# S5 input side by pairs of f tiles, a three-step scan, the skip term on GpSimd, and weight buffers that join the end of the rotation

## The chip, the cores and the metric

One core of a Trainium2 chip runs the whole program in one launch. The metric is device time in microseconds (us); smaller is better. The engines are named as in the profile: PE is TensorE (PEld its weight load), DVE is VectorE, ACT is ScalarE, POOL is GpSimd, and SP issues most DMAs.

## What is computed

Two layers, a gated linear attention (GLA) layer and an S5 layer, on 256 tokens of width 2048, all in float32. The change lies mainly in the S5 layer, whose mixer is, cut to what matters:

```python
proj = u_in @ w_in                      # (256, 2048) @ (2048, 8192)
u, z = jnp.split(proj, 2, axis=-1)      # 256 groups of 16 channels each
# per group g, with 64 complex states and step dt:
lb = exp(a * dt)                        # diagonal transition
bb = (lb - 1) / a * b                   # 64 x 16 input matrix
x[l] = lb * x[l-1] + bb @ u[l]          # complex recurrence along the tokens
y[l] = real(c @ x[l])
y = y + d_skip * u
y = gelu(y)
y = y * sigmoid(y @ w_glu + b_glu)      # (256, 4096) @ (4096, 4096)
out = (y * silu(z)) @ w_out             # (256, 4096) @ (4096, 2048)
```

Around it stand the shift, scale and gate made from the vector c, and a LayerNorm of `ALPHA * x + gate * mixer` after each layer.

## The kernel before, in words

**Dense products.** Each weight comes in blocks of 256 x 512 (`wload`, 512 KB, issued on SP). `split` makes a high part on ACT (`hi`, a rounded copy) and a low part on DVE (`lo = w - hi`), and three fp32r matmuls (hi x hi, hi x lo, lo x hi) stand for one float32 product. The stages of the dense work, by the names of their PSUM tiles, are in this order: v and q (to 377 us of the span), z (377 to 591), op of layer 0 (591 to 771), su (the first half of the S5 `w_in`, 777 to 1052), sz (its second half, 1052 to 1322), gl (`w_glu`, 1325 to 1686), op of layer 1. A group g of su or sz is 512 output columns: four PSUM banks, 8 weight blocks (kp), 192 matmuls of 256 columns.

**Weight buffers.** `ring` is a list of buffer makers. `wload` takes the first and puts it at the end. Four belong to the pool `w`; a phase adds buffers of its own from its temporary pool `tp` (`ring_tmp`), at the front of the list. A pool that is opened where another was closed uses the same memory, so its first tiles wait for the last readers of the closed one's. hi and lo parts have three buffers each.

**The S5 side work** runs between the matmuls of su and sz. An f tile is 8 groups of 16 channels, and there are 32. The recurrence is cut in blocks of 8 tokens:
- `b_pow(f)`: DVE makes the powers of lb times bb (three operations of 128 x 896), from `rb[f // 2]`, which one load brings for two f.
- `b_tr(f)`: eight transposes on PE, copied by ACT to `wbt`.
- `s_in(f)`: a DVE transpose of the su bank, two PE transposes (`psu`), an ACT copy to `U`.
- `s_mm(f)`: eight small float32 matmuls U x wbt (L1014, 32 output partitions each), a DVE transpose of their result into the state array `sx`, then eight more small matmuls c x powers (L1024) into the other half of the same bank, copied by ACT to `kT`.
- `k_out(f)`: two PE transposes (`psk`), an ACT copy to `ks`, on DVE the diagonal skip term `dm` and its sum into `ks`, and a write to the DRAM table `dk` from POOL.
- `scan(c, h)`: one step of the recurrence from block to block, for one half h of the f tiles: four DVE operations of 128 x 128, 30 steps for each half.
- In sz: `cunit(f)` makes two factors wc0 and wc1 (for f % 8 >= 5 DVE adds them to one, L1109), `xstage(f)` transposes the state, and `ystage(f)` sums on PE: eight matmuls with `mt` from `dk`, and eight with each factor of wc.

PSUM has a pool `mm` of five banks for the dense products and `ax` of three for all the rest. `bstep` and `pump` bring in the side work at rates per weight block, and a scheduler then sets the order of the instructions on each engine when the program is built. Each engine and each DMA queue runs its list in that order.

Of the kernel before, what the change touches and what calls it, by code (L numbers as in the profile page):

```python
# [15 lines left out]
P = 128  # L16
# [17 lines left out]
def trunk(ctx, tc, x, c, ln_g, ln_b, ada_w, ada_b, gla_w_in, gla_gate_w2, gla_gate_b, gla_norm_g,  # L34
# [33 lines left out]
    rp.open("rows0")  # L68
    tp = Phase()
# [13 lines left out]
    ones = cp.tile([P, P], F32, name="ones")  # L83
    V.memset(ones, 1.0)
# [18 lines left out]

    last_lo = [None]

    def split(w, name):
        hi = hp.tile([P, 1024], F32R, tag="hi", name="hi" + name)
        lo = lp.tile([P, 1024], F32R, tag="lo", name="lo" + name)
# [10 lines left out]
    def ring_tmp(n):  # L119
        bufs = [lambda name: tp.tile([P, 1024], F32, tag="wx", name=name, bufs=n)] * n  # L120
        ring_add(bufs)
        return bufs[0]

    def ring_drop(buf):
        ring[:] = [b for b in ring if b is not buf]

    def wload(src, k0, c0, name, last=False):
        if last:
            w = wp.tile([P, 1024], F32, tag="w", name="w" + name)
        else:  # L130
            ring.append(ring.pop(0))
            w = ring[-1]("w" + name)
        dma(w.rearrange("p (k c) -> p k c", k=2),
            src[k0 * P:(k0 + 2) * P, c0:c0 + 512].rearrange("(k p) c -> p k c", p=P))
        return w

    def split_last(w, name, i):


        hi = (hp.tile([P, 1024], F32R, tag="hi", name="hi" + name) if i % 2 else lp.tile([P, 1024], F32R, tag="lo", name="hi" + name))  # L140
# [256 lines left out]
    early = ring_tmp(2)  # L397
# [9 lines left out]
    l8r = cp.tile([P, 128], F32, name="l8r")  # L407
    l8i = cp.tile([P, 2, 128], F32, name="l8i")
# [32 lines left out]
    def prep_lambda():  # L441
# [186 lines left out]
    SPLIT = 5  # L628
# [114 lines left out]
    ring_drop(early)  # L743
    tp.close()
    tp.open("tmp0b")
    mid = ring_tmp(4)
# [154 lines left out]
    ring_add(spare)  # L901
# [71 lines left out]
    wu, kts = {}, {}  # L973

    def b_pow(f):
        if f % 2 == 0:
            bload(f // 2)
        a = rb[f // 2][:, f % 2]

        w = tp.tile([P, 8, 16, 8], F32, tag="wu", name=f"wb{f}", bufs=2)  # L980
# [8 lines left out]
        wu[f] = w  # L989

    def b_tr(f):
        wt = tp.tile([P, 8, 128], F32, tag="wbt", name=f"wbt{f}", bufs=2)
        for h in range(2):
            ps = psx(f"pswb{f}{h}")
            for g in range(4):
                PE.transpose(ps[:, g * P:(g + 1) * P], wu[f][:, 4 * h + g].rearrange("p i s -> p (i s)"), ident)
            S.copy(wt[:, 4 * h:4 * h + 4, :], ps.rearrange("p (g r) -> p g r", g=4))
        wb[f] = wt

    def s_in(f, ps):  # L1000
# [8 lines left out]
    def s_mm(f):
        U = Ut[f // 8][:, f % 8]  # L1010
        pss = psx(f"pss{f}")
        for b in range(2):
            for q in range(4):
                PE.matmul(pss[32 * q:32 * q + 32, b * P:(b + 1) * P], lhsT=U[:, b, 32 * q:32 * q + 32],  # L1014
                          rhs=wb[f][:, 2 * q + b, :], start=True, stop=True)
        n = 2 * (f % 16)
        V.transpose(sx[:, f // 16, 1:33, :, n:n + 2].rearrange("p c r b -> p b r c"),
                    pss[:, :T].rearrange("p (b r l) -> p b r l", b=2, r=4))

        cc = rb[f // 2][:, f % 2]  # L1020
        for b in range(2):
            for q in range(4):
                g = 2 * q + b
                PE.matmul(pss[32 * q:32 * q + 32, T + b * P:T + (b + 1) * P], lhsT=cc[:, g * 16:g * 16 + 32],  # L1024
                          rhs=wu[f][:, g].rearrange("p i n -> p (i n)"), start=True, stop=True)
        kt_ = tp.tile([P, 2, P], F32, tag="kt", name=f"kT{f}", bufs=2)
        S.copy(kt_.rearrange("p b (n i) -> p b n i", n=8), pss[:, T:].rearrange("p (b i n) -> p b n i", b=2, i=16))
        kts[f] = kt_

    def k_out(f):  # L1030
        kt_ = kts[f]
        pk_ = psx(f"psk{f}")
        for b in range(2):
            PE.transpose(pk_[:, b * P:(b + 1) * P], kt_[:, b], ident)
        pk = pk_[:, :T].rearrange("p (b q i) -> p q b i", b=2, q=4)[:, :, :, :16]
        ks = tp.tile([P, P], F32, tag="ks", name=f"ks{f}", bufs=1)
        S.copy(ks.rearrange("p (q b i) -> p q b i", q=4, b=2), pk)
        dm = tp.tile([16, 8, 16], F32, tag="dm", name=f"dm{f}", bufs=1)
        V.tensor_tensor(dm, ident[:16, :16].unsqueeze(1).to_broadcast([16, 8, 16]),
                        dT[:, 8 * f:8 * f + 8].unsqueeze(2).to_broadcast([16, 8, 16]), op=ALU.mult)  # L1040
        V.tensor_tensor(ks[:16].rearrange("p (q b i) -> p q b i", q=4, b=2), pk[:16],
                        dm.rearrange("p (q b) i -> p q b i", q=4), op=ALU.add)
        kd = dk[16 * f:16 * f + 16, 896:1920].rearrange("i (n c) -> n i c", n=8)
        wdma(kd, ks)
# [3 lines left out]
    for f in range(35):  # L1048
        if 2 <= f < 34:
            bq.append(lambda f=f: s_mm(f - 2))  # L1050
        if f < 32:
            bq.append(lambda f=f: (b_pow(f), b_tr(f)))
        if f >= 3:
            bq.append(lambda f=f: k_out(f - 3))
# [275 lines left out]
```

## Time and profile before

| What | Value |
|---|---|
| median of 3 runs | 1884.14 us (1879.79 to 1885.82) |
| the profiled execution: its time, its span | 1875.77 us, 1874.0 us |
| PE busy, PEld busy | 1811.6 us (97%), 1582.1 us |
| DVE, ACT, POOL busy | 1441.9 us (77%), 899.1 us (48%), 26.9 us |
| mean granted clock of PE | 0.993 |
| DMA | 449.12 MB, 240 GB/s on average |

The span runs from the first instruction to the last. Busy times of different engines overlap. Two matmuls overlap in the array as well, so the time that one more costs is read from the distance between the starts of two, not from its length. `[0.93 <-ACT hiz L109]` behind a row says that the engine stood idle for 0.93 us before it, until ACT had ended that instruction.

### The profile page before, as it was taken

To read this page: it belongs to the slowest core of one execution; us is meant where nothing else is said; L and a number is where in the kernel's file an instruction comes from. 1 tells how busy PE (TensorE), PEld (TensorE's weight loads), DVE (VectorE), ACT (ScalarE), POOL (GpSimd) and SP (SyncE) were. 2 spreads that over 40 slices of the span, in tenths; PEclk is the share of its full clock that TensorE was granted. 3 is DMA by queue.
4 is the path that set the end of the run, shared out by engine and by line. 5 is a ranking of instruction groups with operands and counts; after the bars stand their busy time and mean duration, and the time that the engine had idled before them with its cause. 6 is when DMAs were issued, how large, how long until landed. Compare 5 with 4: busy or idle time off the path is not lost.

```text
span 1874.0 us, 33634 instructions
## 1 busy us (share of the span) xinstructions
PE 1811.6 (97%) x13443; PEld 1582.1 (84%) x13443; DVE 1441.9 (77%) x2022; ACT 899.1 (48%) x1259; POOL 26.9 (1%) x44
## 2 busy tenths in 40 slices
PE   6999999999999999999999999999899999999997
PEld 3786797899999888898899889898788888888886
DVE  2787675989999888687799879998767775557556
ACT  3533365655556333654454444554544444444332
POOL 0000000000000000000000000000000000000000
PEclk9999999999999999999999999999999999999999
DMA  9978976789888998564555567898678887668653
GB/s 357 321 256 264 354 246 183 230 284 326 287 290 311 342 346 275 168 178 146 165 154 143 167 202 209 221 255 235 212 250 269 270 267 226 190 190 326 192 172 109
DMA packets 239493, 449.12 MB, mean 240 GB/s; under 512 B 19221, under 2 KB 45263, under 8 KB 238055
## 3 DMA queue, kind: packets, MB, share of 16 engines
q1 hardware_dynamic: 235400, 437.53, 73.2%
q0 software_dynamic: 3168, 8.41, 1.4%
q8 instruction: 105, 1.72, 0.4%
q10 hardware_dynamic: 768, 1.05, 0.2%
q14 instruction: 52, 0.42, 0.1%
HBM read 432.49 MB, written 14.42 MB: 238 GB/s over the span
## 4 chain that ended last, share of the span: by engine, by line
PE 64%; issue 9%; DVE 6%; DMA 6%; ACT 1%; POOL 1%; SPq 0%; DVEq 0%; POOLq 0%; ACTq 0%
PE gl L180 13%; PE gl L181 6%; PE op L157 5%; PE op L155 5%; PE op L156 5%; PE z L170 3%; PE z L168 3%; PE z L169 3%; PE su L168 2%; PE su L170 2%; PE su L169 2%; DMA cl<-rec 2%; PE sz L168 2%; PE sz L170 2%; PE sz L169 2%
## 5 line engine op out<-in xcount | busy, mean ns | idle before, releaser
L110 DVE TENSOR_TENSOR logl<-wgl,higl 128x1024 fp32r<-128x1024 f32 x128 | 156.6, 1224 | 118.7 <-ACT higl L109 113.4
L109 ACT CAST higl<-wgl 128x1024 fp32r<-128x1024 f32 x128 | 134.2, 1050 | 177.9 <-PE gl L180 174.6
L180 PE MATMUL gl<-yp,higl 128*128 128x512 f32 x512 | 181.2, 399 | 3.1 <-ACT higl L109 3.1
L180 PE MATMUL gl<-yb,higl 128*128 128x512 f32 x512 | 178.7, 394 | 0.0
L109 ACT CAST hio<-wo 128x1024 fp32r<-128x1024 f32 x96 | 101.3, 1055 | 155.6 <-PE op L157 131.1
L110 DVE TENSOR_TENSOR loo<-wo,hio 128x1024 fp32r<-128x1024 f32 x96 | 117.3, 1224 | 65.6 <-ACT hio L109 63.6
L280 DVE SCALAR_TENSOR_TENSOR acc<-wa,cs,acc 128x512 f32<-128x512 f32 x215 | 160.7, 747 | 4.0 <-DMA wa<-in_ada_w 1.3
L170 PE MATMUL sz<-u1h,losz 128*128 128x256 f32 x512 | 146.5, 287 | 3.9 <-DVE losz L110 3.9
L168 PE MATMUL sz<-u1h,hisz 128*128 128x256 f32 x512 | 149.8, 293 | 0.2 <-ACT zs L1166 0.2
L168 PE MATMUL su<-u1h,hisu 128*128 128x256 f32 x512 | 149.8, 294 | 0.0
L168 PE MATMUL z<-u0h,hiz 128*128 128x256 f32 x512 | 148.7, 290 | 0.9 <-ACT hiz L109 0.9
L170 PE MATMUL su<-u1h,losu 128*128 128x256 f32 x512 | 147.7, 290 | 0.0
L169 PE MATMUL su<-u1l,hisu 128*128 128x256 f32 x512 | 147.1, 287 | 0.0
L170 PE MATMUL z<-u0h,loz 128*128 128x256 f32 x512 | 145.1, 283 | 1.7 <-DVE loz L110 1.7
L169 PE MATMUL sz<-u1l,hisz 128*128 128x256 f32 x512 | 145.5, 284 | 0.0
L169 PE MATMUL z<-u0l,hiz 128*128 128x256 f32 x512 | 144.7, 283 | 0.0
L181 PE MATMUL gl<-yb,logl 128*128 128x256 f32 x512 | 142.7, 279 | 0.0
L181 PE MATMUL gl<-yp,logl 128*128 128x256 f32 x512 | 141.7, 279 | 0.1
L180 PEld LDWEIGHTS gl<-yp,higl 128*128 128x128 f32 x512 | 95.9, 188 | 27.0 <-ACT higl L109 3.3
L180 PEld LDWEIGHTS gl<-yb,higl 128*128 128x128 f32 x512 | 96.0, 187 | 22.4
L155 PE MATMUL v<-hiv,u0h 128*128 128x512 f32 x256 | 103.3, 410 | 5.2 <-ACT u0h L309 2.6
L109 ACT CAST hiz<-wz 128x1024 fp32r<-128x1024 f32 x64 | 67.1, 1053 | 83.8 <-PE z L169 78.4
(319 smaller groups left out, 4965.8 us busy)
## 6 DMA issues: line engine op xcount, KB each, us to landing
wgl<-in_s_w_glu SPq DMA_DIRECT2D x128, 512.0 KB, 4.7
wa<-in_ada_w SPq DMA_DIRECT2D x115, 512.0 KB, 5.1
a<-in_ada_w SPq DMA_DIRECT2D x32, 1024.0 KB, 11.4
wv<-in_gla_w_in SPq DMA_DIRECT2D x64, 512.0 KB, 6.1
wz<-in_gla_w_in SPq DMA_DIRECT2D x64, 512.0 KB, 5.1
wsu<-in_s_w_in SPq DMA_DIRECT2D x64, 512.0 KB, 3.9
wsz<-in_s_w_in SPq DMA_DIRECT2D x64, 512.0 KB, 5.3
wo<-in_s_w_out SPq DMA_DIRECT2D x64, 512.0 KB, 4.6
```

Of the source, the lines that this page charges most:

```text
L109: S.copy(hi, w)
L110: last_lo[0] = V.tensor_tensor(lo, w, hi.bitcast(F32), op=ALU.subtract).ins
L155: PE.matmul(banks[tt], lhsT=uh, rhs=hi[:, kk, :], start=(k == first), stop=False)
L156: PE.matmul(banks[tt], lhsT=uh, rhs=lo[:, kk, :], start=False, stop=False)
L157: PE.matmul(banks[tt], lhsT=ul, rhs=hi[:, kk, :], start=False, stop=(k == last))
L168: PE.matmul(o, lhsT=wh, rhs=u.hi(k), start=(k == first), stop=False)
L169: PE.matmul(o, lhsT=wh, rhs=u.lo(k), start=False, stop=False)
L170: PE.matmul(o, lhsT=wl, rhs=u.hi(k), start=False, stop=(k == last))
L180: PE.matmul(banks[f], lhsT=hi[:, kk, fs], rhs=u.both(k), start=(k == 0), stop=False)
L181: PE.matmul(banks[f][:, :T], lhsT=lo[:, kk, fs], rhs=u.hi(k), start=False, stop=(k == last))
L280: V.scalar_tensor_tensor(acc[0], w[:, kk, :], cs[:, k:k + 1], acc[0], op0=ALU.mult, op1=ALU.add)
```

## The change

1. **Pairs.** `s_mm`, `k_out` and the second half of `s_in` take two f at once (p stands for f // 2). `s_mm` takes two `ax` banks and issues 8 + 8 matmuls for the first f and 8 + 8 for the second, with both DVE transposes and both copies after all 32. The powers and their transposes get a tile for each pair, from the pool `s8`.
2. **Skip on POOL.** `dm` and its sum into `ks` are POOL operations of 16 x 256, one of each for a pair, on SBUF alone.
3. **Scan of three steps.** The constants `l8` hold the real and the signed imaginary part side by side. One multiplication of 128 x 256 takes the place of two of 128 x 128, and two sums follow.
4. **No sum of wc0 and wc1.** `ystage` takes both factors for all 32 f.
5. **Rings.** hi and lo have rings as well. `more` puts a phase's own buffers at the end of a ring. During su and the first group of sz there is one weight, one hi and one lo buffer more.
6. The constant `ones` and the tiles `zs` are made where a pool has room for them.

The core of the diff:

```diff
-    ring = [lambda name: wp.tile([P, 1024], F32, tag="w", name=name)] * 4
-    def ring_add(bufs):
-        ring[0:0] = bufs
...
+        def add_tmp(self, tag, dt, n):
+            bufs = [lambda name: tp.tile([P, 1024], dt, tag=tag, name=name, bufs=n)] * n
+            self.extend(bufs)
...
-    early = ring_tmp(2)
+    early = more(2, 0)
...
-    mid = ring_tmp(4)
+    mid = more(4, 0)
...
+    def s_mm(p):
+        pss = [psx(f"pss{2 * p + i}") for i in range(2)]
+        for i in range(2):
...
+            for b in range(2):
+                for q in range(4):
+                    PE.matmul(pss[i][32 * q:32 * q + 32, b * P:(b + 1) * P], lhsT=U[:, b, 32 * q:32 * q + 32],
+                              rhs=wb[p][:, i, 2 * q + b, :], start=True, stop=True)
+            for b in range(2):
+                for q in range(4):
+                    g = 2 * q + b
+                    PE.matmul(pss[i][32 * q:32 * q + 32, T + b * P:T + (b + 1) * P], lhsT=cc[:, g * 16:g * 16 + 32],
+                              rhs=wu[p][:, i, g].rearrange("p i n -> p (i n)"), start=True, stop=True)
+        kt_ = tp.tile([P, 2, 2, P], F32, tag="kt", name=f"kT{p}", bufs=1)
+        for i in range(2):
+            V.transpose(sx[:, f // 16, 1:33, :, n:n + 2].rearrange("p c r b -> p b r c"),
+                        pss[i][:, :T].rearrange("p (b r l) -> p b r l", b=2, r=4))
+            S.copy(kt_[:, i].rearrange("p b (n i) -> p b n i", n=8), pss[i][:, T:].rearrange("p (b i n) -> p b n i", b=2, i=16))
...
+        nc.gpsimd.tensor_tensor(dm, ident[:16, :16].unsqueeze(1).to_broadcast([16, 16, 16]),
+                                dT[:, 16 * p:16 * p + 16].unsqueeze(2).to_broadcast([16, 16, 16]), op=ALU.mult)
+        kv = ks[:16].rearrange("p f c -> p (f c)")
+        nc.gpsimd.tensor_tensor(kv, kv, dm.rearrange("p g i -> p (g i)"), op=ALU.add)
...
-        V.tensor_tensor(t1, X, lr.unsqueeze(1).to_broadcast([P, 2, 2, 32]), op=ALU.mult)
-        V.tensor_tensor(t2, X[:, ::-1], li, op=ALU.mult)
-        V.tensor_tensor(t1, t1, t2, op=ALU.add)
-        V.tensor_tensor(N, N, t1, op=ALU.add)
+        V.tensor_tensor(t1, X.unsqueeze(1).to_broadcast([P, 2, 2, 64]), l8[:, h], op=ALU.mult)
+        V.tensor_tensor(t1[:, 0], t1[:, 0], t1[:, 1, ::-1], op=ALU.add)
+        V.tensor_tensor(N, N, t1[:, 0], op=ALU.add)
...
-        if f % 8 >= SPLIT:
-            V.tensor_tensor(w[0], w[0], w[1], op=ALU.add)
-            w.pop()
...
+            if (g, kp) == (0, 3):
+                mid = more(1, 1)
...
-    ring_tmp(4)
+    more(4, 0)
```

What the scheduler makes of it, at the places of which the prediction speaks. First PE at the start of the second weight block of group 3 of su. su30 to su33 are the four banks of the dense product, pss8 and pss9 the banks of the small matmuls of f = 8 and 9. Before:

```order
L170 MATMUL su33_8762<-u1h0_7394,losu30_8766 128x256
L1014 MATMUL pss8_8793<-wbt8_8605,U1_7519 32x128 x8
L169 MATMUL su30_8759<-u1l0_7396,hisu31_8815 128x256
L170 MATMUL su30_8759<-u1h0_7394,losu31_8816 128x256
L168 MATMUL su30_8759<-u1h0_7394,hisu31_8815 128x256
L169 MATMUL su30_8759<-u1l0_7396,hisu31_8815 128x256
L170 MATMUL su30_8759<-u1h0_7394,losu31_8816 128x256
L1024 MATMUL pss8_8793<-wb8_8599,rb4_8595 32x128 x8
```

The same place in the changed kernel:

```order
L181 MATMUL su33_8706<-u1l0_7396,hisu30_8709 128x256
L182 MATMUL su33_8706<-u1h0_7394,losu30_8710 128x256
L1038 MATMUL pss8_8737<-wbt4_8582,U1_7519 32x128 x8
L1043 MATMUL pss8_8737<-wb4_8576,rb4_8572 32x128 x8
L1038 MATMUL pss9_8738<-wbt4_8582,U1_7519 32x128 x8
L1043 MATMUL pss9_8738<-wb4_8576,rb4_8572 32x128 x8
L180 MATMUL su30_8703<-u1h0_7394,hisu31_8778 128x256
```

Four blocks of small matmuls (two for pss8 here, two for pss9 further on) have become one. Counted over su and sz, the small matmuls of `s_mm` stand in 64 blocks between dense matmuls before, and in 16 now. The transposes and the psy matmuls stand in 111 blocks before and in 137 now, because the transposes of `b_tr` now come four at a time.

Second, SP at the change from the v stage to the z stage. wz00 to wz03 are the first weight blocks of z, wa belong to the modulation vectors. Before:

```order
L133 DMA wz02_3554<-in_gla_w_in 128x2x512
L133 DMA wa0205_3584<-in_ada_w 128x2x512
L133 DMA wz03_3595<-in_gla_w_in 128x2x512
L133 DMA wa0206_3625<-in_ada_w 128x2x512
L133 DMA wz00_3472<-in_gla_w_in 128x2x512
L133 DMA wa0203_3502<-in_ada_w 128x2x512
L133 DMA wz01_3513<-in_gla_w_in 128x2x512
```

Now:

```order
L136 DMA wz00_3472<-in_gla_w_in 128x2x512
L136 DMA wa0203_3502<-in_ada_w 128x2x512
L136 DMA wz01_3513<-in_gla_w_in 128x2x512
L136 DMA wa0204_3543<-in_ada_w 128x2x512
L136 DMA wz02_3554<-in_gla_w_in 128x2x512
L136 DMA wa0205_3584<-in_ada_w 128x2x512
L136 DMA wz03_3595<-in_gla_w_in 128x2x512
```

The blocks that PE needs first are now issued first: they go to buffers of the pool `w`, and the new phase's own buffers come later.

Third, SP at the change from sz to gl; mt29 to mt31 are the last `mt` tiles. Before:

```order
L133 DMA wgl05_15110<-in_s5_w_glu 128x2x512
L1099 DMA cl31_14765<-rec_182 128x256
L1101 DMA cl31_14765<-rec_182 64x128
L1118 DMA mt30_14693<-dk_183 128x1x1024
L1101 DMA cl31_14765<-rec_182 64x128
L1118 DMA mt31_14769<-dk_183 128x1x1024
L133 DMA wgl06_15134<-in_s5_w_glu 128x2x512
L133 DMA wgl07_15158<-in_s5_w_glu 128x2x512
L133 DMA wgl00_14990<-in_s5_w_glu 128x2x512
L133 DMA wgl01_15014<-in_s5_w_glu 128x2x512
```

Now:

```order
L136 DMA wgl00_14780<-in_s5_w_glu 128x2x512
L1143 DMA mt29_14384<-dk_183 128x1x1024
L136 DMA wgl01_14804<-in_s5_w_glu 128x2x512
L1127 DMA cl31_14530<-rec_182 128x256
L1129 DMA cl31_14530<-rec_182 64x128 x2
L1143 DMA mt30_14459<-dk_183 128x1x1024
L136 DMA wgl02_14828<-in_s5_w_glu 128x2x512
L1143 DMA mt31_14534<-dk_183 128x1x1024
L136 DMA wgl03_14852<-in_s5_w_glu 128x2x512
```

wgl00 to wgl03 have moved ahead of the last loads of the sz stage; wgl04 to wgl07 now stand behind them and behind wgl08 and wgl09.

## Rows read from the trace of the kernel before

**Rows 1.** Busy time by stretch: span from:to, PE, PEld, DVE, ACT, POOL, clock, DMA.

```profile
777.00:1052.20 275.20, 272.57 (x2796) 249.27 (x2796) 236.03 (x402) 142.14 (x263) 15.51 (x26) 0.99 0.55 160
950.00:1052.20 102.20, 101.73 (x1081) 92.12 (x1080) 100.62 (x224) 49.88 (x91) 7.14 (x12) 1.00 0.54 153
1110.00:1321.60 211.60, 200.38 (x2602) 187.10 (x2600) 197.04 (x295) 108.03 (x168) 0.00 (x0) 0.99 0.84 227
```

**Rows 2.** Timeline of PE in su: start, length, instruction.

```profile
906.77 0.28 PE L170 MATMUL su<-u1h,losu 128*128 128x256 f32 x1
906.98 0.65 PE L1014 MATMUL pss<-wbt,U 128*32 128x128 f32 x16
907.55 0.39 PE L168 MATMUL su<-u1h,hisu 128*128 128x256 f32 x1
907.78 0.28 PE L169 MATMUL su<-u1l,hisu 128*128 128x256 f32 x1
```

**Rows 3.** The same view where transposes stand between dense matmuls.

```profile
903.28 0.28 PE L168 MATMUL su<-u1h,hisu 128*128 128x256 f32 x1
903.40 1.04 PE L996 MATMUL pswb<-ident,wb 128*128 128x128 f32 x8
...
904.62 0.28 PE L170 MATMUL su<-u1h,losu 128*128 128x256 f32 x1
...
913.74 0.28 PE L169 MATMUL su<-u1l,hisu 128*128 128x256 f32 x1
913.85 0.41 PE L1005 MATMUL psu<-ident,vv 128*128 128x128 f32 x2
...
914.22 0.28 PE L168 MATMUL su<-u1h,hisu 128*128 128x256 f32 x1
```

**Rows 4.** Timeline in sz: a psy block with two factors, and with one.

```profile
1302.11 0.43 PE L1141 MATMUL psy<-mt,U 128*32 128x128 f32 x8
...
1303.56 0.39 PE L168 MATMUL sz<-u1h,hisz 128*128 128x256 f32 x1
...
1306.85 0.42 PE L1141 MATMUL psy<-mt,U 128*32 128x128 f32 x8
...
1307.86 0.39 PE L168 MATMUL sz<-u1h,hisz 128*128 128x256 f32 x1
```

**Rows 5.** Groups by line, shapes apart: busy us, mean ns of one, idle before.

```profile
L1109 DVE TENSOR_TENSOR wc<-wc,wc 128x1024 f32<-128x1024 f32 x12 | 14.3, 1188 | 0.0
L1070 DVE TENSOR_TENSOR sca<-sx,l8r 128x128 f32<-128x128 f32 x60 | 16.7, 278 | 1.2 <-DMA dk<-ks 0.9
L1041 DVE TENSOR_TENSOR ks<-psk,dm 16x128 f32<-16x128 f32 x32 | 8.8, 274 | 2.1 <-ACT ks L1037 2.0
L1220 DVE TENSOR_TENSOR sg<-gl,sg 128x256 f32<-128x256 f32 x32 | 12.7, 416 | 0.8 <-ACT sg L1219 0.8
masks.py:199 POOL TENSOR_SCALAR_AFFINE_SELECT ident<-ident 128x128 f32<-128x128 f32 x1 | 0.3, 288 | 0.1
```

**Rows 6.** Timeline at the start of z.

```profile
375.89 1.04 ACT L109 CAST hiz<-wz 128x1024 fp32r<-128x1024 f32 x1 [2.28 <-DMA wz<-in_gla_w_in]
376.98 0.38 PE L168 MATMUL z<-u0h,hiz 128*128 128x256 f32 x1 [0.93 <-ACT hiz L109]
378.24 0.39 PE L170 MATMUL z<-u0h,loz 128*128 128x256 f32 x1 [0.76 <-DVE loz L110]
```

**Rows 7.** Timeline at the start of gl.

```profile
1323.66 1.04 ACT L109 CAST higl<-wgl 128x1024 fp32r<-128x1024 f32 x1 [0.45 <-DMA wgl<-in_s_w_glu]
1324.76 1.20 PE L180 MATMUL gl<-yp,higl 128*128 128x512 f32 x4 [3.06 <-ACT higl L109]
```

**Rows 8.** Waits of PE and DVE in sz, from 1090 us: total, times, longest.

```profile
PE psxs L1129 <- DVE xT L1126: 8.8, 3, 3.9
DVE wc L971 <- DMA cl<-rec: 9.1, 5, 3.7
PE sz L170 <- DVE losz L110: 3.1, 1, 3.1
```

More of the change, by code (lines that the diff above doesn't have):

```diff
@@ L101, in pump, with take, drop, more @@
                 bg.pop(0)()
+    class Ring(list):
+        def take(self, name):
+            self.append(self.pop(0))
+            return self[-1](name)
+        def drop(self, buf):
+            self[:] = [b for b in self if b is not buf]
+        def add_tmp(self, tag, dt, n):
+            bufs = [lambda name: tp.tile([P, 1024], dt, tag=tag, name=name, bufs=n)] * n
+            self.extend(bufs)
+            return bufs[0]
+    ring = Ring([lambda name: wp.tile([P, 1024], F32, tag="w", name=name)] * 4)
+    his = Ring([lambda name: hp.tile([P, 1024], F32R, tag="hi", name=name)] * 3)
+    los = Ring([lambda name: lp.tile([P, 1024], F32R, tag="lo", name=name)] * 3)
+    def more(nw, nh):
+        got = [(ring, ring.add_tmp("wx", F32, nw))]
+        for r, tag in ((his, "hx"), (los, "lx")):
+            if nh:
+                got.append((r, r.add_tmp(tag, F32R, nh)))
+        return got
+    def less(got):
+        for r, b in got:
+            r.drop(b)
+    def wload(src, k0, c0, name, last=False):
+        w = wp.tile([P, 1024], F32, tag="w", name="w" + name) if last else ring.take("w" + name)
+        dma(w.rearrange("p (k c) -> p k c", k=2),
+            src[k0 * P:(k0 + 2) * P, c0:c0 + 512].rearrange("(k p) c -> p k c", p=P))
+        return w
     last_lo = [None]
     def split(w, name):
-        hi = hp.tile([P, 1024], F32R, tag="hi", name="hi" + name)
-        lo = lp.tile([P, 1024], F32R, tag="lo", name="lo" + name)
+        hi = his.take("hi" + name)
+        lo = los.take("lo" + name)
         S.copy(hi, w)
@@ L111, in split @@
         return hi.rearrange("p (k c) -> p k c", k=2), lo.rearrange("p (k c) -> p k c", k=2)
-    ring = [lambda name: wp.tile([P, 1024], F32, tag="w", name=name)] * 4
-    def ring_add(bufs):
-        ring[0:0] = bufs
[L119 to L135, printed above, removed]
     def split_last(w, name, i):
-        hi = (hp.tile([P, 1024], F32R, tag="hi", name="hi" + name) if i % 2 else lp.tile([P, 1024], F32R, tag="lo", name="hi" + name))
+        hi = (his if i % 2 else los).take("hi" + name)
         lo = (tp.tile([P, 1024], F32R, tag="wx", name="lo" + name, bufs=4) if i < 4 else
@@ L627, in trunk @@
     KEEP = (4, 6)
-    SPLIT = 5
     GATE_AT = 15
@@ L1009, in s_mm @@
[L1009 to L1044, printed above, removed]
@@ L1047, in trunk, with s_in @@
-    bq = []
[L1048 to L1054, printed above, removed]
+                PE.transpose(ps[:, g * P:(g + 1) * P], wu[p][:, f % 2, 4 * h + g].rearrange("p i s -> p (i s)"), ident)
+            S.copy(wb[p][:, f % 2, 4 * h:4 * h + 4, :], ps.rearrange("p (g r) -> p g r", g=4))
+    def s_in(p, banks):
+        v = tp.tile([P, 2, 2, 16, 8], F32, tag="vv", name=f"vv{p}", bufs=2)
+        for i in range(2):
+            V.transpose(v[:, i].rearrange("p b i s -> p s b i"),
+                        banks[i][:, :T].rearrange("p (s b i) -> p s b i", s=8, b=2)[:, ::-1])
+        return v
@@ L1056, in trunk @@
+    bq = []
+    for p in range(18):
+        if 1 <= p < 17:
+            bq.append(lambda p=p: s_mm(p - 1))
+        for f in (2 * p, 2 * p + 1):
+            if f < 32:
+                bq.append(lambda f=f: (b_pow(f), b_tr(f)))
+        if p >= 2:
+            bq.append(lambda p=p: k_out(p - 2))
     b_pace = [0.0]
@@ L1088, in trunk @@
             pump(SCAN_RATE)
-        for i in range(4):
-            s_in(4 * g + i, banks[i])
+        vs = [s_in(2 * g + i, banks[2 * i:2 * i + 2]) for i in range(2)]
+        for i in range(2):
+            s_in2(2 * g + i, vs[i])
         if g == 4:
@@ L1153, in cside @@
         cunit(f)
-    zs = [s8t(f"zs{i}", [8, T]) for i in range(4)]
+    zs = []
     for g in range(8):
```

91 lines of the change are left out of this document (56 added, 35 removed).

## The prediction

> **What bounds the kernel now.** I read the busy times by stretch first, because the change touches only some of them. PE is the bound almost everywhere, in su as well: 272.6 of 275.2 us busy, while DVE has 236 and ACT 142 [rows 1]. In the last hundred microseconds of su DVE is full too (100.6 of 102.2), and PE still hardly waits. In sz both are close to full: PE stands idle for 11.2 of 211.6 us from 1110 on, DVE for 14.6. So DVE work that goes is worth something only where PE waits for DVE. What counts is what PE has to do, and that I read from its timeline.
>
> A busy share of 99% does not say that PE does only useful work. In [rows 2] two dense matmuls that are normally 0.12 us apart (903.28 and 903.40 in [rows 3]) have eight small ones between them: from 906.77 to 907.78 are 1.01 us for two dense steps and the eight, so these cost 1.01 - 0.24 = 0.77 us. In sz a psy block with two factors (24 small matmuls) takes 1303.56 - 1302.11 = 1.45 us, one with a single factor (16) takes 1.01 [rows 4]. Eight more in the same block therefore cost 0.44. The other 0.33 of the 0.77 is the price of going from dense to small matmuls and back. Transposes do not pay it: ten cost 1.34 - 0.24 = 1.10, two cost 0.48 - 0.24 = 0.24 [rows 3], which is 0.11 each and about 0.02 for a block.
>
> **The change part by part**, against the profiled execution's 1875.8 us.
>
> *Small matmuls of s_mm in one block for a pair.* The order shows 64 blocks before and 16 after, with the same 512 matmuls. 48 x 0.33 = 15.8 us of PE time go, all of it on the path, since PE is the bound there. Bounds: 0, if the fixed cost belongs to each group of eight, and 48 x 0.57 = 27, if it is more than I read; psy, which mixes two sources of operands in one block without a gap [rows 4], is the nearest row, so I take 15.8.
>
> *Transposes in more blocks:* 137 - 111 = 26 x 0.02 = +0.5.
>
> *No sum of wc0 and wc1:* 12 f get eight more matmuls, 12 x 0.44 = +5.3 on PE. DVE loses 12 operations, 14.3 us [rows 5].
>
> *Scan and skip:* a scan step had four operations of 0.278 and gets one of about 0.416 (a 128 x 256 row) and two of 0.278, so 60 x 0.14 = 8.4 us of DVE go. `dm` and its sum were 64 operations of about 0.27, 17.3 us [rows 5]. In su this is worth nothing by itself, because PE covers it. I take 1 us of the 2.6 in which PE is idle there. In sz PE is idle for 11.2 us after 1110 and 3.1 before that. 8.8 of this is a wait for the transpose xT on DVE and 3.1 one for a low part [rows 8]. Only a part of it is DVE's load: DVE itself waits 9.1 us for the loads `cl`, which stand in one SP queue behind others, and that does not change. Bounds: all 14.3 gone, or 5 more; I take -5.
>
> *Rings, z.* The first cast of z waits 2.28 us for its weights, and PE behind it 0.93 and 0.76 [rows 6]. Now wz00 to wz03 use buffers that are free earlier, and they are first in the queue. Nothing else is late there, since the psst matmuls and their copies are done. Bounds 0 and -1.7, I take -1.5.
>
> *Rings, gl.* PE waits 3.06 us for the first high part, whose weights had just landed [rows 7], because wgl00 needed the memory of the sz stage's tiles. It is now issued before the last `cl` load. What is late next: gl02 needs the bank of sz71, and ACT now has the last gelu, and so two more table loads, between the Silu of sz70 and that of sz71; PE has two banks of work meanwhile. wgl04 to wgl07 stand behind wgl08 and wgl09, which wait for the low parts of wgl00 and wgl01, but they are needed only four blocks later. Bounds 0 and -3.06, I take -2.5.
>
> *POOL.* Two operations for a pair wait for ACT's copy, and behind them on POOL stand only the two writes of the same pair. Nothing but the `dk` loads of sz waits for those. What hides them is the whole stage, since one pair lasts some 17 us of su (275.2 / 16). Their own length is not in the trace. The only operation of that kind on POOL is 128 elements wide and takes 0.288 [rows 5]; twice the elements and two inputs give 0.29 to 1.15.
>
> *Extra buffers, `ones`, `zs`:* 0. They are behind none of the waits listed here, and where a buffer more lets a load start sooner, PE is still busy with the block before.
>
> Sum: -15.8 + 0.5 + 5.3 - 1 - 5 - 1.5 - 2.5 = -20.0, or 1855.8 for an execution like the profiled one. The three runs shown have a median 8.4 us above the profiled one, so the forecast on their scale is 1884.1 - 20.0 = **1864**.
>
> **Rivals.**
>
> *A. The 0.33 belongs to eight matmuls, not to a block.* For it: all blocks of `s_mm` in this trace have the same size, so I can't see one grow. Against it: psy grows by 0.44 for eight. Then -20.0 + 15.8 = -4.2, or 1880: no change that can be measured.
>
> *B. The pair's banks come free too late: slower.* The pair takes two of three `ax` banks, and the DVE transposes of both come after all 32 matmuls. In the order PE has 24 dense matmuls, four transposes in the third bank and 9 dense ones, 33 x 0.12 + 0.44 = 4.4 us, before it needs the first of the two again. If DVE is further behind than that, PE stands. DVE is full from 950 on [rows 1], over some seven pairs. At 4 us late in each this is 28 us, and 1884 + 28 - 20 = 1892. It decides from 20 / 7 = 2.9 us late in each. Against it: before, PE waited for these banks nearly never with the same DVE load, and DVE's load falls.
>
> *C. POOL stops DVE.* Each POOL operation would hold up a DVE operation with two SBUF operands (the low parts, powers and scans all have them) for its whole length. At 1.15 us, 12 of them in the full stretch cost 14 us of DVE, against some 6.5 freed by the skip and 4 by the scan there. PE, which is to get through that stretch 5 us sooner, would lose about 8: -12, or 1872. The trace shows no POOL arithmetic beside DVE, so it speaks neither for nor against. This is what the Trainium skill states in "SBUF — State Buffer", section "Who interferes with whom": a DVE instruction with two SBUF inputs and a GpSimd instruction that reads SBUF shut each other out for a whole instruction. No run here shows it yet. For the length, "GPSIMD Engine Reference", section "Elementwise — side-by-side cycle accounting", has about 2.6 cycles for each element of a two-input operation; at its 1.2 GHz that makes an estimate of 0.55 us for 256, and by that C would cost PE next to nothing.
>
> **How the numbers follow.** Forecast 0.68, A 0.12, B 0.09, C 0.11. The forecast's own range is 1853 to 1874: -11 if neither the waits in sz nor those at the two starts go, -31 if they all go and some more of the block cost does. Below it I leave little. Above it I go to 1882, which takes in A and C and leaves out B: **1852 to 1882**. About 0.3%, 5.7 us, is what a measurement of this kernel can tell from no change. Faster than 1878.5 is nearly all of the forecast, most of C and a third of A: 0.80. Within the band is the rest of A and a piece of C: 0.10. Slower is B and what else could go wrong with the order: 0.10.
>
> **What would show it.** Right: a block of 32 small matmuls takes about 4 x 0.44 + 0.33 = 2.1 us between dense matmuls, su is some 14 us shorter, DVE has some 40 us less to do, no wait of PE at the start of gl longer than 1 us. A: the block takes 3.1. B: PE waits for DVE's sx transposes before pswb. C: DVE's low parts in su get longer in the moments when POOL works. sz is the least certain term: it is wrong if PE waits there as long as before, in which case sz is 4 us longer, not the same. The whole is wrong if su is not at least 8 us shorter.

## The result, and the profile after

The kernel after takes 1860.2 us (median of four runs, 1856.07 to 1863.56), the kernel before on the same chip 1884.98: a ratio of 0.9866, with a 95% interval of 0.9836 to 0.9897, or 25 us less. The forecast was 1864 in a range of 1852 to 1882. The two profiled executions differ by 19.7 us in their spans (1874.0 and 1854.3): the one of the kernel before ran at a mean granted clock of 0.993, while 24 others of it, beside which later runs were measured, had 0.983 to 0.992, so against its stages a gain reads small. The total came out as forecast. The parts of it did not, and the rest of this text is about that.

Stage by stage, from the first dense matmul of one to the first of the next, in us. The wait at the start of a stage counts in the stage ahead of it, and all stages ahead of z are one column:

| kernel | to z | z | op | su | sz | gl | op2 to end |
|---|---|---|---|---|---|---|---|
| before | 377.0 | 214.7 | 185.5 | 275.1 | 272.5 | 361.8 | 187.4 |
| after | 375.6 | 213.6 | 185.4 | 270.5 | 260.6 | 361.0 | 187.6 |

So su gave 4.6 us, where the prediction has some 14 (56 of its 64 blocks of small matmuls stand in su), and sz with the start of gl gave 11.9, where its terms give about 4. The busy times of the kernel after by stretch (columns as in [rows 1]: su, sz, the first 4 us around the start of gl, and the start of z):

```profile
774.50:1045.00 270.50, 263.49 (x2803) 250.10 (x2803) 236.70 (x325) 137.39 (x250) 48.76 (x49) 0.99 0.55 168
1045.00:1302.00 257.00, 251.56 (x3260) 237.75 (x3261) 218.50 (x299) 130.82 (x205) 12.19 (x15) 0.99 0.81 220
1302.00:1306.00 4.00, 4.00 (x54) 3.76 (x47) 4.00 (x7) 3.81 (x6) 0.00 (x0) 1.00 0.20 49
...
360.00:384.00 24.00, 24.00 (x178) 20.96 (x177) 22.00 (x29) 12.10 (x25) 1.15 (x1) 1.00 0.95 319
```

PE no longer waits at the two starts (the third and the last row, against [rows 6, 7]). In su PE's busy time fell by 9.1 us against [rows 1], but its idle time grew from 2.6 to 7.0. DVE is as busy in su as it was (236.7 and 236.0).

The new block of small matmuls on PE's timeline (start, length, instruction), to be held against [rows 2]:

```profile
908.27 0.28 PE L182 MATMUL su<-u1h,losu 128*128 128x256 f32 x1
908.48 0.65 PE L1038 MATMUL pss<-wbt,U 128*32 128x128 f32 x16
908.94 0.62 PE L1043 MATMUL pss<-wb,rb 128*32 128x128 f32 x16
909.38 0.62 PE L1038 MATMUL pss<-wbt,U 128*32 128x128 f32 x16
909.82 0.62 PE L1043 MATMUL pss<-wb,rb 128*32 128x128 f32 x16
910.37 0.39 PE L180 MATMUL su<-u1h,hisu 128*128 128x256 f32 x1
910.59 0.28 PE L181 MATMUL su<-u1l,hisu 128*128 128x256 f32 x1
```

From 908.27 to 910.59 are two dense steps of 0.12 and the 32: 2.32 - 0.24 = 2.08, against the 2.1 forecast. (Eight small matmuls stand as x16, as in [rows 2].) 64 x 0.77 became 16 x 2.08, which is 16.0 us less, 14.0 of it in su (56 blocks became 14). The block term is right to a fifth of a microsecond, and still su gave only 4.6. What was late instead shows on ACT's and PE's timeline:

```profile
898.79 0.66 ACT L994 COPY wb<-rb 128x128 f32<-128x128 f32 x2 [2.03 <-DMA rb<-rec]
...
899.25 0.63 ACT L1011 COPY wbt<-pswb 128x512 f32<-128x512 f32 x1
...
899.94 0.66 PE L1010 MATMUL pswb<-ident,wb 128*128 128x128 f32 x4 [0.68 <-ACT wbt L1011]
```

ACT's queue is in order. The copy of rb for the next pair waits 2 us for its load, and the copy wbt that empties a bank stands behind it, so the third group of transposes waits for the bank. Over all of su (waits of ACT, PEld and PE, and of SP's queue: total, times, longest):

```profile
ACT wb L994 <- DMA rb<-rec: 13.4, 6, 3.1
...
PEld pswb L1010 <- ACT wbt L1011: 8.6, 25, 1.5
...
PE pswb L1010 <- ACT wbt L1011: 3.7, 4, 1.3
PE psu L1025 <- DVE vv L1017: 2.3, 5, 1.3
...
SPq L968 <- PE pss L1043: 15.9, 6, 4.5
```

The last row says why the load is late: rb has two buffers of one pair each, and the load must wait until the block of 32 that reads the old buffer is done. The kernel before had the first of these waits once, with 1.4 us.

### The profile page after: what moved, and what is told of

Read it like the earlier page. It is cut to its first block, busy times and chain, and to the rows that moved or that the text cites. A ratio compares the mean times of both kernels' runs of the same rounds, so it can differ in the third digit from the quotient of the medians.

```text
span 1854.3 us, 33845 instructions
## 1 busy us (share of the span) xinstructions
PE 1802.9 (97%) x13635; PEld 1587.3 (86%) x13635; DVE 1423.6 (77%) x1886; ACT 894.9 (48%) x1247; POOL 68.8 (4%) x76
## 4 chain that ended last, share of the span: by engine, by line
PE 70%; DVE 8%; DMA 4%; issue 2%; ACT 1%; SPq 0%; DVEq 0%; ACTq 0%
PE gl L192 13%; PE gl L193 6%; PE op L168 6%; PE op L169 6%; PE op L167 6%; PE z L182 3%; PE z L180 3%; PE z L181 3%; PE sz L180 3%; PE sz L182 2%; PE sz L181 2%; PE su L180 2%; PE su L181 2%; PE su L182 2%; DMA rb<-rec 1%
## 5 line engine op out<-in xcount | busy, mean ns | idle before, releaser
L145 ACT CAST hisz<-wsz 128x1024 fp32r<-128x1024 f32 x64 | 66.9, 1050 | 100.9 <-PE sz L181 66.2
L145 ACT CAST hisu<-wsu 128x1024 fp32r<-128x1024 f32 x64 | 66.8, 1049 | 92.8 <-PE su L181 79.7
```

## The experiments

Each was compared with the kernel before on the same chip. Theory T1 is the chain just read: rb, ACT's queue, the bank. Rival T2 is GpSimd: its two operations hold VectorE up, and VectorE is what PE waits for.

**Split rb.** The columns that the powers read stay in rb; the 144 columns that the small matmuls read get a tile of their own, loaded after the block of the pair before.

```diff
-        a = tp.tile([P, 2, 512], F32, tag="rb", name=f"rb{f2}", bufs=2)
-        dma(a[:, :, 0:384], rec[:, 2 * f2:2 * f2 + 2, :])
+        a = tp.tile([P, 2, 384], F32, tag="rb", name=f"rb{f2}", bufs=2)
+        dma(a[:, :, 0:256], rec[:, 2 * f2:2 * f2 + 2, 128:384])
...
+        rc[f2] = tp.tile([P, 2, 144], F32, tag="rc", name=f"rc{f2}", bufs=2)
+        dma(rc[f2], rec[:, 2 * f2:2 * f2 + 2, 0:144])
...
-            cc = rb[p][:, i]
+            cc = rc[p][:, i]
```

> The kernel after, with the rb tile split in two: the columns that the powers read (128 to 383 and the swapped half) stay in rb with two buffers, the 144 columns that the small matmuls read go to a tile of their own, loaded one pair ahead. So rb is free as soon as the powers are done and its load no longer waits for the block of 32 matmuls. Theory T1 (the su stage gave 4.5 us instead of 16 because ACT's in-order queue stands at the copy of rb, so the copy that frees a bank comes late and TensorE waits before the third pswb block): the waits of PE and PEld on the wbt copy (12.3 us together after) fall under 4 us, su falls from 270.5 to 263 to 266 us, the total to about 1854 us (ratio to before about 0.983). Rival T2 (VectorE is held up by GpSimd's two operations and is what TensorE waits for): the ACT waits move to waits on VectorE, su stays within 2 us of 270.5, ratio 0.986 to 0.987.

Measured: 1855.02 us, ratio 0.9839 (0.9818 to 0.986), su 267.3, sz 258.8. ACT's wait for rb is there once, and PEld's waits for wbt are all short:

```profile
ACT wb L1001 <- DMA rb<-rec: 2.7, 1, 2.7
...
PEld pswb L1017 <- ACT wbt L1018: 5.1, 26, 0.2
```

The chain is gone, and su is 3.2 us shorter in the profiled executions. That is less than T1 gave (4.5 to 7.5), and the waits for wbt are 5.1 us and not under 4. The intervals of this ratio and of the kernel after overlap. T1 is a part of the answer.

**The skip term on VectorE.**

```diff
-        nc.gpsimd.tensor_tensor(dm, ident[:16, :16]...
+        V.tensor_tensor(dm, ident[:16, :16]...
-        nc.gpsimd.tensor_tensor(kv, kv, dm...
+        V.tensor_tensor(kv, kv, dm...
```

> The kernel after, with the two operations of the skip term (dm and its sum with ks) on VectorE instead of GpSimd, as before the change. T2 (GpSimd's use of the SBUF holds VectorE up): the mean low part in su falls from 1283 ns back to about 1211 ns, VectorE's busy time in su from 236.7 to about 236 in spite of 32 more small operations, su falls by 2 to 5 us. T1: the ACT waits stay, su stays within 1.5 us of 270.5 or grows by 1 to 4 us since VectorE issues 16 x 2 operations more. The terms of my prediction say that the skip on GpSimd is worth nothing on the path that sets the end.

Measured: 1856.84 us, ratio 0.9856 (0.9832 to 0.988), su 270.2. The low parts in su (busy, mean ns), of the kernel after and then of this one, and the operation on GpSimd in the kernel after:

```profile
L146 DVE TENSOR_TENSOR losu<-wsu,hisu 128x1024 fp32r<-128x1024 f32 x62 | 79.3, 1283 | 14.2 <-ACT hisu L145 14.1
...
L1068 POOL TENSOR_TENSOR ks<-ks,dm 16x256 f32<-16x256 f32 x12 | 21.4, 1786 | 189.9 <-ACT ks L1062 189.9
```

```profile
L146 DVE TENSOR_TENSOR losu<-wsu,hisu 128x1024 fp32r<-128x1024 f32 x62 | 75.1, 1215 | 14.8 <-ACT hisu L145 14.4 <-PE pss L1043 0.3
...
L1068 DVE TENSOR_TENSOR ks<-ks,dm 16x256 f32<-16x256 f32 x16 | 6.4, 401 | 3.2 <-ACT ks L1062 3.2
```

The half of T2 that speaks of the hold is shown: without GpSimd's arithmetic a low part takes 1215 ns again, against 1283. The other half is not: su did not get shorter, because VectorE now does the work itself (0.4 us an operation), and it is as busy in su as before the edit (236.6 and 236.7 us).

**Both together.**

> Split rb and the skip term on VectorE together. T1 alone: su as in the run with split rb alone (263 to 266 us), no further gain. T2 alone: su as with the skip on VectorE alone. If both take part, the gains add: su near the 259 us that the prediction's sum gives (275.0 less 16), the total about 1849 us (ratio about 0.981).

Measured: 1851.39 us, ratio 0.9815 (0.9793 to 0.9838), su 264.3, sz 262.4. This is below the kernel after, and it is the lowest median here. Its busy times in su:

```profile
776.20:1040.50 264.30, 262.66 (x2804) 249.80 (x2803) 238.70 (x352) 137.91 (x250) 14.22 (x24) 1.00 0.59 173
```

PE is idle for 1.6 us. Each edit by its profile gave 3.2 and 0.3 in su, both 6.2: with the loads on time VectorE's delay by GpSimd is the next thing that PE waits for (PE's waits for `vv` on VectorE are 2.3 us with split rb alone and 0.3 here). The totals do not decide it: the two kernels differ by 4.5 us (+-6), and sz is 3.6 us longer in this profile. Of the 14 us forecast for su 10.8 are now there. Added up from PE's timeline, the small blocks of transposes in su took 41 us before, 54 in the kernel after and 47 here, while the forecast had +0.5. A group of four pswb transposes that does not wait takes 0.44 us. Of the 52 such groups in su 26 take that here, and the other 26 take 0.65, each with one of the short waits for wbt that the run ahead shows too. One of them (ACT's cast, ACT's copy, PE's weight load):

```profile
867.00 1.05 ACT L145 CAST hisu<-wsu 128x1024 fp32r<-128x1024 f32 x1 [1.08 <-PE su L181]
...
867.96 0.58 ACT L1018 COPY wbt<-pswb 128x512 f32<-128x512 f32 x1
...
868.59 0.42 PEld L1017 LDWEIGHTS pswb<-ident,wb 128*128 128x128 f32 x4 [0.20 <-ACT wbt L1018]
```

26 x 0.21 are 5.5 us, most of what is left between 47 and 41. In all 26 the copy runs on ACT straight behind a cast of a weight block. Whether a fourth bank, or the copy ahead of the cast, would take these waits away, no run tried.

**The buffers at the front of the rotation.**

```diff
-            self.extend(bufs)
+            self[0:0] = bufs
```

> The kernel after, with a phase's own weight buffers put at the front of the rotation again, as before. By the prediction's two terms for it the start of z gets later by 1.5 us (0 to 1.7) and the start of gl by 2.5 us (0 to 3.06), so the total is 4 us longer (ratio about 0.989). Rival: at gl TensorE waits for something else in place of the load (the wait of 3 us comes back elsewhere, or the small work of sz hides it): then z alone is later, total 1.5 us longer, and op2 starts as before.

Measured: 1882.9 us, ratio 0.9985 (0.9972 to 0.9998). In this kernel the order of the buffers decides over nearly all the gain, some 22 us instead of 4. Of this 13.5 us are in su (284.0), 4.7 in sz with the start of gl, 2.2 up to the start of z, where kernels that all have the buffers at the end differ as much (375.1 to 377.8 us). The timeline at the start of the side work of su (all engines), and the windows around it:

```profile
794.65 0.37 SPq L968 DMA_DIRECT2D rb<-rec  x1
...
799.04 0.65 ACT L994 COPY wb<-rb 128x128 f32<-128x128 f32 x2 [3.99 <-DMA rb<-rec]
...
800.91 1.04 ACT L145 CAST hisu<-wsu 128x1024 fp32r<-128x1024 f32 x1 [1.22 <-DMA wsu<-in_s_w_in]
...
802.01 0.58 PE L180 MATMUL su<-u1h,hisu 128*128 128x256 f32 x1 [8.14 <-ACT hisu L145]
```

```profile
794.00:802.00 8.00, 0.00 (x0) 0.00 (x0) 4.96 (x6) 2.74 (x5) 0.61 (x1) 0.80 0.91 280
802.00:812.00 10.00, 9.37 (x53) 9.11 (x54) 6.79 (x7) 2.22 (x3) 0.00 (x0) 0.65 0.29 91
812.00:822.00 10.00, 9.93 (x85) 9.73 (x84) 7.05 (x9) 5.66 (x9) 0.00 (x0) 1.00 0.59 166
```

PE does nothing for 8 us, and the granted clock is 0.65 on the mean over the 10 us behind that (between its levels of 1.2 and 2.4 GHz), then 1.00 again. So an idle stretch is paid twice: the 0.65 is worth about 3.5 us (10 x 0.35, an estimate). In all of su PE was idle for 8.4 us more than in the kernel after, and busy for 5.1 us more; a second stretch at the lower level, at 986 us, has a part in the 5.1. When PE stopped it had used four weight blocks (96 dense matmuls of su) and ACT had cast seven: the fifth block, which PE needed next, was cast behind later ones.

**The same without the extra buffers of su**, which the kernel before does not have:

```diff
-            if (g, kp) == (0, 3):
-                mid = more(1, 1)
```

> The kernel after with its buffers at the front, and without the extra buffers of su (one weight, one high and one low buffer). Theory: of the 22.7 us that the front costs, 13.5 come from su's extra weight buffer alone: it lies in memory that the making of u1 still uses, so at the front the next load must wait for it, TensorE stalls for 8.1 us and then runs at a lower granted clock. Without that buffer su falls from 284.0 to 270 to 272 us and the total to about 1866 us (ratio about 0.990), with z and gl later than in the kernel after by about 1.5 and 3 us. Rival (the front order costs su through the old buffers as well): su stays above 278 us.

Measured: 1871.87 us, ratio 0.9938 (0.9916 to 0.9959), su 273.3. 10.7 of the 13.5 us in su are gone with the extra buffers, so the most of it does come from them; su is 1.3 us and the total 6 above what was expected. The weight, high and low buffer were taken out together, so that it is the weight buffer alone is not shown. Nor is it shown that the load waited for the memory of the making of u1: SP's one wait for `u1l` in su is 7.6 us with the extra buffers and without them.

**The kernel after without the extra buffers of su** (the same edit, with the buffers at the end):

> The kernel after without the extra buffers of su. The prediction gave these buffers no gain: su stays at 270 to 271 us, ratio 0.986 to 0.987. Rival: they keep ACT's casts ahead of the copies that wait for rb; without them su grows by 3 us or more (ratio 0.988 or above).

Measured: 1862.98 us, ratio 0.9892 (0.986 to 0.9924), su 271.4, sz 261.6. The point is 5 us above the kernel after, the interval of that difference about +-8 (roots of the sums of squares here and below). In su it is 0.9 us. The ratio lies where the rival put it, su does not. Nothing speaks against the zero of the prediction, and gains of a few microseconds are not excluded. Between this kernel and the one above, which differ by the order alone, are 8.7 us (+-7).

**The rotation alone, in the kernel before.**

```diff
-        ring[0:0] = bufs
+        ring.extend(bufs)
```

> The kernel before with one edit: a phase's own weight buffers join the end of the rotation (the spare buffers of op stay at the front). It is the rotation part of the change alone, without pairs, scan, skip or extra buffers. The prediction's two terms: z starts 1.5 us earlier, gl 2.5 us earlier, su unchanged: 4 us, ratio about 0.998. Rival: the 22.7 us that the kernel after loses with its buffers at the front are what the rotation is worth by itself; then this kernel is some 20 us faster than before (ratio about 0.989), with a shorter su.

Measured: 1877.72 us, ratio 0.9966 (0.9951 to 0.9982), which is 6.4 us (3.4 to 9.2). PE's wait at the start of gl is gone and z takes 213.6 as in the kernel after. In its profile sz, with the wait at gl gone, is still 276.8 us, 4.3 more than in that of before: PE waited for xT for 11.8 us there, and the granted clock in sz was 0.96 (0.99 before). The prediction's 4 us lie inside, the rival's 20 do not.

**Blocks of sixteen, in the kernel before:** both eights of one f in one block.

```diff
-        V.transpose(sx[:, f // 16, 1:33, :, n:n + 2]...
         cc = rb[f // 2][:, f % 2]
         for b in range(2):
...
+        V.transpose(sx[:, f // 16, 1:33, :, n:n + 2]...
```

> The kernel before with one edit: in s_mm the transpose into sx is issued behind the second eight matmuls, so both eights of one f stand together and 64 blocks of eight become 32 blocks of sixteen. By the prediction's price of a block (0.33 us besides its matmuls) TensorE has 32 x 0.33 = 10.6 us less in su and sz; since the kernel before waits little in su, su falls by 7 to 10 us and the total to 1875 us (ratio about 0.995). Rival A (0.33 us belongs to each eight matmuls): no change, a block of sixteen takes 1.54 us. Rival D (in su what ends last is not TensorE's own time but the chain of rb, ACT and the banks): the blocks get shorter, but su by less than 4 us, the rest comes back as waits.

Measured: 1886.85 us, ratio 1.0017 (0.9998 to 1.0035). PE's timeline, and its busy time in su:

```profile
905.32 0.28 PE L170 MATMUL su<-u1h,losu 128*128 128x256 f32 x1
905.53 0.65 PE L1014 MATMUL pss<-wbt,U 128*32 128x128 f32 x16
905.99 0.62 PE L1020 MATMUL pss<-wb,rb 128*32 128x128 f32 x16
906.54 0.39 PE L168 MATMUL su<-u1h,hisu 128*128 128x256 f32 x1
906.76 0.28 PE L169 MATMUL su<-u1l,hisu 128*128 128x256 f32 x1
```

```profile
776.80:1051.00 274.20, 268.51 (x2796) 249.93 (x2795) 235.24 (x401) 145.00 (x262) 15.53 (x26) 1.00 0.55 160
```

1.44 - 0.24 = 1.20 for sixteen: the price of 0.33 for a block holds (2 x 0.44 + 0.33 = 1.21), and rival A falls again. But su got only 0.9 us shorter: idle time grew from 2.6 to 5.7 us, and a block of eight pswb and two psk transposes went from a median of 1.09 to 1.33. That is rival D. Without other changes the merged blocks gave nothing. In sz this profile is 6.5 us longer than that of before, with 1.5 us more of waiting for xT and 2.0 for the low part at a clock of 0.98; why is not settled, but the run above, which has the same work in sz, had 276.8 there, so it need not be the edit.

**The sums of wc0 and wc1 back in the kernel after,** for 12 of the 32 f:

```diff
+        if f % 8 >= 5:
+            V.tensor_tensor(w[0], w[0], w[1], op=ALU.add)
+            w.pop()
```

> The kernel after with the sum of wc0 and wc1 for 12 of the 32 f again, as before: VectorE gets 12 x 1.19 = 14.3 us in sz, TensorE loses 12 x 0.44 = 5.3 us. Theory S (sz gave 11.9 us instead of the 4.2 that I took, with the start of gl, because TensorE's waits in sz came from VectorE's load and the sums were most of it): the waits for xT and the low part come back, sz grows from 260.6 to 263 to 269 us in spite of the 5.3 us less on TensorE, ratio 0.988 to 0.991. Rival (the waits went for another reason: the scan, the rotation, the bigger blocks): sz falls by 3 to 5 us, ratio about 0.984.

Measured: 1869.58 us, ratio 0.9918 (0.9903 to 0.9933), sz 271.7. PE's and DVE's waits in sz:

```profile
PE psxs L1157 <- DVE xT L1154: 9.5, 3, 4.1
...
DVE wc L982 <- DMA cl<-rec: 14.6, 5, 4.9
```

and those of the kernel after:

```profile
PE psxs L1154 <- DVE xT L1151: 0.7, 2, 0.4
...
DVE wc L982 <- DMA cl<-rec: 4.2, 3, 1.6
```

Theory S holds in kind; 271.7 and 0.9918 lie above its ranges. PE was idle for 11.8 us more in sz than in the kernel after, and busy for only 0.7 less although it lost 5.3 us of work: the granted clock was 0.97 there, against 0.99. Where the waits come from shows on the timeline of DVE and PE in the kernel with the sums:

```profile
1206.57 1.23 DVE L982 TENSOR_TENSOR wc<-cl 128x1024 f32<-128x1024 f32 x1 [4.19 <-DMA cl<-rec]
...
1210.97 0.44 PE L1157 MATMUL psxs<-ident,xT 128*128 128x128 f32 x2 [2.59 <-DVE xT L1154]
...
1306.91 1.23 DVE L982 TENSOR_TENSOR wc<-cl 128x1024 f32<-128x1024 f32 x1 [4.89 <-DMA cl<-rec]
...
1311.42 0.66 PE L1157 MATMUL psxs<-ident,xT 128*128 128x128 f32 x2 [4.08 <-DVE xT L1154]
```

All three long waits of PE for xT (1211, 1264, 1311 us) come 2 to 4.5 us behind a DVE product that waited for its cl load, in the stretches of the f that sum. In the kernel after no wait for cl is longer than 1.6 us, and PE does not wait behind one.

**No sums, in the kernel before** (line 1108 of it, `>= SPLIT` made `>= 8`).

> The kernel before with one edit: no f sums wc0 and wc1, so all 32 have the 48 matmuls; the sums' part of the change alone. Theory S: sz falls by 2 to 6 us from 272.5 (TensorE 5.3 us more, its 15.8 us of waits there mostly gone), ratio about 0.998. Rival (the sums alone do not free it, since the scan, the small matmuls' blocks and the start of gl remain): sz grows by 1 to 5 us, ratio about 1.001.

Measured: 1875.55 us, ratio 0.9951 (0.9938 to 0.9964), which is 9.2 us less from this edit alone; sz 268.8, with PE busy for 258.0 instead of 254.8. The two profiles have the same span (1874.1 and 1874.0) and differ by 3.7 us in sz. The six executions of this kernel ran at a granted clock of 0.992 to 0.993, the ten of the kernel before that stood beside them at 0.987 to 0.991, so a part of the 9.2 is the clock. The waits in sz, to be held against [rows 8]:

```profile
PE psxs L1129 <- DVE xT L1126: 1.3, 2, 1.0
...
DVE wc L970 <- DMA cl<-rec: 3.4, 5, 1.3
DVE wc L971 <- DMA cl<-rec: 1.5, 2, 0.9
```

8.8 us of PE's waiting for xT became 1.3, and the waits of the two products for cl fell from 9.9 together to 4.9, the longest from 3.7 to 1.3. PE works longer and the stage is shorter.

**A scan of four operations in the kernel after.**

```diff
-        V.tensor_tensor(t1, X.unsqueeze(1).to_broadcast([P, 2, 2, 64]), l8[:, h], op=ALU.mult)
+        for j in range(2):
+            V.tensor_tensor(t1[:, j], X, l8[:, h, j], op=ALU.mult)
```

> The kernel after with the wide product of a scan step split into two of half the width, so that a step has four operations again: VectorE gets 60 x 0.14 = 8.4 us, half of it in su, half in sz. By the prediction: su within 1 us of 270.5 if VectorE is hidden there; in sz up to 4 us more. Ratio 0.986 to 0.989. Rival (the scan is what freed sz): sz at 265 us or above.

Measured: 1863.09 us, ratio 0.9888 (0.987 to 0.9906): 4 us (+-7) above the kernel after. The profile has 3.6 us more in su and 2.7 in sz, which at 263.3 stays below the 265 of the rival. That VectorE is hidden in su (within 1 us) was missed in this profile; the total does not decide it.

**Both edits, and the loads of mt from GpSimd's queue.**

```diff
-        dma(m.rearrange("p t g i -> p (t g i)"), src)
+        wdma(m.rearrange("p t g i -> p (t g i)"), src)
```

> Split rb and the skip term on VectorE (the fastest so far), and the loads of mt in sz issued by GpSimd's queue instead of SyncE's, where 11.4 us of waiting for psy stand ahead of the weight and cl loads. If TensorE's last waits in sz (4.2 us for mt) come from that order, sz falls from 262.4 to 256 to 259 us and the total to about 1847 us (ratio about 0.979). Rival: the loads' issue on GpSimd costs VectorE or is later than on SyncE; sz stays at 261 us or grows (ratio 0.981 or above).

Measured: 1852.69 us, ratio 0.9816 (0.9796 to 0.9836), sz 263.8. A miss: the waits for mt are gone, and PE waits 4.2 us for xT instead of 1.7.

## Why the total was right, and which steps were wrong

The prediction names its own test: "The whole is wrong if su is not at least 8 us shorter." su was 4.6 us shorter. By that test the working failed. The total came out by luck, because two errors cancelled: su gave 9 us less than forecast, sz with the start of gl 8 more. And the prediction has no term for the clock: the executions of the kernel after ran at 0.991 to 0.994 (mean 0.9928), the 24 of the kernel before named above at 0.9888 on the mean, and 0.004 x 1875 gives an estimate of some 7 us of the 25.

| part | forecast, us | measured alone, us (95%) |
|---|---|---|
| pairs: small blocks, transposes | -15.3 | su -4.6 in the kernel after; blocks of 16 alone +3.2 (-0.4 to +6.6) |
| sums of wc0 and wc1 | +5.3, and a share of the -5 in sz | -9.2 (-11.7 to -6.8); back in the kernel after: +9.8 (+-6) |
| rotation | -4.0 | -6.4 (-9.2 to -3.4) |
| scan | a share of -1 and of -5 | back in the kernel after: +4 (+-7) |
| skip on GpSimd | 0 | back on VectorE: -2 (+-7) |
| extra buffers | 0 | taken out: +5 (+-8) |

*Small matmuls.* The price of a block is right (2.08 for 2.1, and 1.20 for 1.21). The failed step is the sentence "all of it on the path, since PE is the bound there", with its neighbour "26 x 0.02 = +0.5" for the transposes. PE was 99% busy in su, but only because the banks, their copies and the loads came just in time. When the blocks got cheaper, the waits for banks came in their place: 41 us of transposes became 54. The experiment with rb and the skip shows two causes of it, late rb loads and GpSimd, which together hold 6.2 us by the profiles; the third, the 26 short waits for ACT's copies (5.5 us), was read from the rows and not tried. I had costed rb's load nowhere, though the pair makes its buffer free later.

*Rival B* had the right place, banks that come free too late, and the wrong cause: no wait of PE for VectorE's sx transposes is in the list of waits, the banks were late through ACT. And it was worth some 10 us, not 28.

*Sums.* The term was right in its pieces (psy blocks with 24 matmuls are 1.86 with xT's transposes where those with 16 are 1.43; DVE lost 12 operations of 1.19). The failed step is "DVE itself waits 9.1 us for the loads `cl` [...] and that does not change". With the sums alone taken out the long ones went (3.7 to 1.3), and with them PE's waits; with the sums back in the kernel after they came again (4.9). A reading that fits both: the buffer of cl comes free only when VectorE has done its products, so a VectorE that is late makes the next load late and waits for it in turn. I had the rows of both waits [rows 8] and took the one for a cause that VectorE's load can't touch. A row of SP's queue shows the tie from VectorE to the load, in the kernel with the sums and in the kernel after (SP's waits at the first load of a cl, in sz):

```profile
SPq L1127 <- DVE yt L1175: 52.1, 28, 3.9
...
SPq L1127 <- DVE yt L1172: 55.9, 28, 3.9
```

SP stands there until VectorE has ended an operation, but no longer with the sums than without. And the load for which VectorE waits 4.89 us at 1306.9 had been issued at 1297.8 at the latest, 9 us ahead. So that this loop, and not the order of SP's queue or a slow transfer, makes the long waits is argued, not shown. The clock of 0.97 in sz has a share in the 9.8 us.

*Rotation.* Both waits went as forecast: in the kernel after PE waits neither at the start of z (0.93 and 0.76 us before) nor at gl (3.06), and z takes 1.1 us less. The time at which z starts says little (377.0 and 375.6), since kernels of the new order have 375.1 to 377.8. The size is in the interval.

*Skip and GpSimd.* Rival C's mechanism is there. The Trainium skill, "SBUF — State Buffer", section "Who interferes with whom", says that a VectorE instruction with two SBUF inputs contends with a GpSimd instruction that reads SBUF, and that the lock is exclusive; the trace agrees: a low part that began 0.67 us before the end of GpSimd's 1.68 us operation took 1.76 us instead of 1.21 (the rows stand below). By its profile it costs the kernel after nothing, as forecast, because the skip on VectorE costs as much; but by the profiles it costs 3 us of su once rb is on time. VectorE's 40 us less were 18 (1441.9 to 1423.6 us over the whole span), of which 14.3 are the sums: by its rows the scan gave 5.2 us instead of 8.4, and low parts and powers grew by 7, which the run with the skip on VectorE does not show.

## What to carry to other kernels

An engine that is 99% busy is the bound only as far as its neighbours are early: before a saving on it is counted, look how much slack the copies, banks and loads have that feed it, and shorten it in thought until the first of them is late. Work taken from an engine that is not the bound can still be worth much, where the bound waits for it at times (14.3 us of VectorE gave 9.2, a part of it by the clock, while TensorE got 5.3 more), so a wait of one engine for a load and a wait of another for that engine should be read together before one of them is called fixed. A new buffer is safer at the end of a rotation: at the front it takes the very next block, and here that block came behind later ones and TensorE stood for 8.1 us.

## What the runs showed of the hardware

GpSimd's and VectorE's operations with two SBUF inputs hold each other up. From the kernel after, start and length:

```profile
905.87 1.68 POOL L1068 TENSOR_TENSOR ks<-ks,dm 16x256 f32<-16x256 f32 x1 [12.82 <-ACT ks L1062]
...
906.88 1.76 DVE L146 TENSOR_TENSOR losu<-wsu,hisu 128x1024 fp32r<-128x1024 f32 x1
...
957.92 5.39 POOL L1068 TENSOR_TENSOR ks<-ks,dm 16x256 f32<-16x256 f32 x1 [15.02 <-ACT ks L1062]
...
1072.63 0.73 POOL L1068 TENSOR_TENSOR ks<-ks,dm 16x256 f32<-16x256 f32 x1 [1.58 <-ACT ks L1062]
```

The same 16 x 256 sum takes 0.40 us on VectorE. On GpSimd it takes 0.73 where VectorE does nothing beside it (the last row), and 1.79 on the mean in su, more than the 1.15 that I had as its upper bound. The 5.39 us are a sum beside which VectorE ran eight two-input operations in a row (957.55 to 962.71), all at their usual lengths; it ended at 963.31, when VectorE had gone on to a transpose out of PSUM. So the delay goes both ways, and GpSimd's can be the longer one. The prediction's estimate of 0.55 us is near the shortest of these operations (0.61 for `dm`, 0.72 for the sum), not near the mean.

And one idle stretch of 8 us of TensorE was followed by 10 us at a granted clock of 0.65, which cost about 3.5 us more (the estimate above).
